# A decoder layer on one core: the up projection's outputs in two sets, each tile convolved a tile later, a copy on another engine, four row-by-row steps at the end

## The chip, the core and the metric

The kernel runs on one core of a Trainium2 chip. The core has a matrix engine, TensorE (PE in the profile, its weight loads PEld), and three engines for elementwise work: VectorE (DVE), ScalarE (ACT) and GpSimd (POOL). SyncE (SP) issues nearly all transfers between the chip's memory and the core's on-chip memory; a matmul's result lands in one of eight accumulator banks, from which DVE or ACT fetch it. Each engine works through its own instructions in order and waits on semaphores for the others. The metric is the time of one execution in microseconds, the median of three runs.

## The reference

One layer of a hybrid decoder in float32, on 1024 tokens behind 16 meta tokens, with 1024 columns: a combined input projection, four heads of differential attention and four heads of a gated linear recurrence, an output projection, and then a feed-forward part with a convolution, which is most of the work:

```python
def conv_ffn(a, w_up, conv_w, conv_b, w_down):
    u = a @ w_up                                  # 1024 -> 2 * 2816
    u = lax.conv_general_dilated(u, conv_w[:, None, :], window_strides=(1,),
        padding=[(CONV_WIDTH - 1, 0)], dimension_numbers=('NWC', 'WIO', 'NWC'),
        feature_group_count=C) + conv_b           # 3 taps along the tokens
    gate, up = jnp.split(u, 2, axis=-1)
    return (jax.nn.gelu(gate, approximate=True) * up) @ w_down

    # in the layer
    mix = jnp.concatenate([y_diff, y_hgrn], axis=-1) @ w_out[l]
    h = h + rmsnorm(mix, ln_mix_post[l])
    a = rmsnorm(h, ln_ffn_pre[l])
    h = h + rmsnorm(conv_ffn(a, ...), ln_ffn_post[l])
```

In the attention, each block of 128 queries forms two softmaxes p0 and p1 over the keys so far, and (p0 − λ·p1) is multiplied by the values.

## The kernel before

**Precision and products.** Each operand of a float32 product is split into a high part, cast to a fast 32-bit matmul type by ACT, and a low remainder, which DVE or POOL form by subtraction. A product is then three matmuls, high by high, high by low, low by high: L1412 to L1414 in the up phase, L1586 to L1588 in the down phase. Both phases use a 2 × 2 block scheme with seven block products in place of eight.

**Stages.** Up to about 490 us the input projections run between the heads: a projection, an attention head's blocks and the recurrence's steps are generators that a planner interleaves. Until 646 us the output projection, its norm and the transposed, split tokens follow. Then come 22 tiles of the up phase (ft = 0 to 21, each 128 gate columns and 128 up columns), to 1064.85 us, and last the down phase, 77 steps: seven products in the order 1, 2, 5, 6, 3, 7, 4 of 11 steps each, a step being four rows of three matmuls with 512 columns.

**A tile of the up phase.** `unit(ft, p)` is a generator with one yield for each of its seven products, and two units, p = 0 and 1 for the two token halves, run side by side. Product j of a unit is 12 matmuls into one of three banks in turn: pa, pb, pc, pb, pa, pb, pc. What fetches a bank is named by its result: ACT copies pa to x1 (in the profile xu) and to ug; DVE adds pb to x1 for u2 (xu), pb to x1 for u3 (u), pc to u3 and pb to x1 for the two halves of uu, pc to u2 for the second half of ug. `outputs(ft, p)` gives the buffers ug and uu (gate and up); `gated` convolves them: for each side, `conv` runs one ACT instruction and two scalar-tensor-tensor instructions on DVE (c<-ug and c<-uu), then ACT makes the GELU, POOL multiplies the two sides, and SP stores the row block to gsc in the chip's memory. `later` is a list of tiles' halves that are still to be convolved; the loop over ft takes one from it at j = 1 and one at j = 3, behind that product's last addition (an order edge, `issue_after`, that only sets the order on one engine).

In the kernel before, tiles 1 and 2 take their outputs from buffers that the down phase owns (tags gk, gh, gl) and leave their convolutions to the next tile; tile 3 and all later ones take them from the pool xu and convolve at their own end, at j = 6. Tile 0, which is made in a plain way, leaves its convolutions to tile 1.

Beside this, `prep` makes the next tile's weights: `load_raw4` loads four blocks ra, POOL forms sums of them (ws), ACT casts the high parts uh, and DVE and POOL form the low ones ul.

**Down phase.** `operands` loads (gi from gsc, wi from the weights) and splits both into gh, gl, wh, wl, three steps ahead. The first three pairs of loads (`opens`) are issued in tile 20, at j = 5, behind the last gsc store so far, and split in tile 21. For products 1 to 7 all four rows (m = 0 to 3, one bank each) are summed step by step; in the last one, product 4, the last `TAIL` steps are done row by row, so that row 0 can be fetched, normed and stored while the others are still summed. `evac` does that: a subtraction from the bank on DVE, the squares and the root on ACT, a multiplication by the gain and one or two scalar-tensor-tensor instructions into hh on DVE, for rows 0 to 2 also one addition on POOL, and a store of the row block.

**Attention.** `values(i)` transposes the softmax block i in pieces of four 128-blocks to a bank (pt) and copies each piece to the tile at, by DVE or ACT in turn; `apply(i)` multiplies them by the values (L746).

**Order.** PE's matmuls keep the order in which the program writes them. The other engines' instructions are put in order by a scheduler, so a diff of a few lines can move many of them. All elementwise instructions are recorded under one helper's line, L58; they are told apart by their tiles.

Of the kernel before, what the change touches and what calls it, by code (L numbers as in the profile page):

```python
# [9 lines left out]
F32 = mybir.dt.float32  # L10
# [7 lines left out]
P = 128  # L18
# [3 lines left out]
D = 1024  # L22
KD = D // P
DFF = 2816
NF = DFF // P
HEADS = 4
NBLK = 9
# [63 lines left out]
def layer_kernel(ctx: ExitStack, tc: tile.TileContext, x, meta, table, lbl, gpre, gpost, win,  # L91
# [3 lines left out]
    V, A = Ordered(tc, nc.vector, state), Ordered(tc, nc.scalar, state)  # L95
# [552 lines left out]
    def attn(h, tens):  # L648
# [60 lines left out]
        def values(i):  # L709
            r = rows(i)  # L710
            q0 = start(i)
            W = q0 + r
            nm = f"{h}_{i}"
            pb = pend.pop(i)
            pieces = [list(range(j, min(j + 4, i + 1))) for j in range(0, i + 1, 4)]
            ats = []
            for pi, blks in enumerate(pieces):
                pt = ps_m(f"pt{nm}_{pi}")
                at = ap_.tile([P, len(blks) if pi == 2 else 4, P], F32, tag=f"at{pi // 2}", name=f"at{nm}_{pi}", bufs=2 - pi // 2)
                for jj, j in enumerate(blks):  # L720
                    b = rows(j) if i == 0 else P
                    T.transpose(pt[:b, jj * r:(jj + 1) * r], pb[:r, 0, start(j):start(j) + b], ident[:r, :r])
                pv = pt.rearrange("p (j q) -> p j q", j=4)[:, :, :r] if r == P else None
                n0 = len(blks)
                if pi == 0:
                    A.copy(az[i % 2][:META, :r], pt[:META, :r])
                lo = 1 if pi == 0 else 0
                if n0 > lo:
                    (A.copy if pi % 2 else V.tensor_copy)(at[:, lo:n0], pv[:, lo:n0])
                ats.append(at)  # L730
                yield 0.8 if i < 4 else 0.6
            pend["ats"] = ats, pieces
# [323 lines left out]
        return mix_tile(tag, F32R, f"mp{n}_{i}")[:, : 2 * KD * P].rearrange("p (l k t) -> p l k t", l=2, k=KD)  # L1056

    def block_load(m, i, k0, k1):
        SY.dma_start(m[:, :, k0:k1].bitcast(F32).rearrange("p l k t -> p l (k t)"), msc[i][:, :, P * k0:P * k1])

    def first_load(i):
        blocks[i] = block_tile(0, i)
        block_load(blocks[i], i, 0, 4)
        block_load(blocks[i], i, 4, 7)

    def second_load(i):
        blocks[i] = block_tile(1, i)
        block_load(blocks[i], i, 0, 4)
        block_load(blocks[i], i, 4, 7 if i == 1 else 8)

    blocks = {}
    first_load(1)
    first_load(2)
    wo0 = load_wo(0)
    wo0_loaded = last_load[-1]
    SY.dma_start(gpo0, gpost[:, :512].to_broadcast([P, 512]))

    def y0_gain(p):
# [59 lines left out]
    def load_raw4(ft):  # L1138
        raws.clear()
        for nm, m, c in (("11", ft, 0), ("22", ft + NF, 1), ("21", ft + NF, 0), ("12", ft, 1)):  # L1140
            raws[nm] = swp.tile([P, 512], F32, tag="ra", name=f"ra{ft}_{nm}", bufs=5)
            with tc.issue_after(wo0_loaded.ins):
                SY.dma_start(raws[nm], wup[m][:, 512 * c: 512 * (c + 1)])

    def w_sum(nm, a, b, op):
# [208 lines left out]
    gap(tp, "gap1", 128)  # L1354

    def outputs(ft, p):
        if ft in (1, 2):
            if p == 0:
                return [dn.tile([P, 2 * WN[0]], F32, tag="gk", name=f"{t}{ft}_{p}") for t in ("ug", "uu")]
            return [dn.tile([P, 512], F32R, tag=g, name=f"{t}{ft}_{p}").bitcast(F32) for g, t in (("gh", "ug"), ("gl", "uu"))]  # L1360
        return [xup.tile([P, 2 * WN[0]], F32, tag=t, name=f"{t}{ft}_{p}") for t in ("ug", "uu")]
# [35 lines left out]
    def unit(ft, p, bank):  # L1397
        n = WN[p]
        nm = f"{ft}_{p}"
        ug, uu = outputs(ft, p)  # L1400
        if (ft, p) == (1, 0):
            gap(dn, "gap7", 384)
        pair = mxp.tile([P, 768], F32, tag="ms", name=f"xu_{nm}", bufs=2)
        x1, u2 = pair[:, :n], pair[:, WN[0]:WN[0] + n]
        u3 = xup.tile([P, WN[0]], F32, tag="u3", name=f"u3_{nm}")[:, :n]

        def mm(j, pt, first):
            hi, lo = made[7 * ft + j]
            th, tl = tt[p][j]
            for k in range(4):  # L1410
                s = slice(P * k, P * (k + 1))
                T.matmul(pt, hi[:, s], th[:, k], start=(first and k == 0), stop=False, skip_group_check=True)  # L1412
                T.matmul(pt, hi[:, s], tl[:, k], start=False, stop=False, skip_group_check=True)  # L1413
                T.matmul(pt, lo[:, s], th[:, k], start=False, stop=(k == 3), skip_group_check=True)  # L1414

        pa = bank(f"pa{nm}")[:, :n]
        mm(0, pa, True)
        marks["x1"] = A.copy(x1, pa)
        yield
        pb = bank(f"pb{nm}")[:, :n]  # L1420
        mm(1, pb, True)
        marks[ft, p] = marks["last"] = V.tensor_tensor(u2, pb, x1, op=ALU.add)
        yield
        pc = bank(f"pc{nm}")[:, :n]
        mm(2, pc, True)
        yield
        mm(3, pb, False)
        V.tensor_tensor(u3, pb, x1, op=ALU.add)
        marks["last"] = V.tensor_tensor(uu[:, n:2 * n], pc, u3, op=ALU.add)
        yield  # L1430
        mm(4, pa, False)
        marks["left"] = A.copy(ug[:, :n], pa)
        yield
        mm(5, pb, False)
        marks["last"] = V.tensor_tensor(uu[:, :n], pb, x1, op=ALU.add)
        yield
        mm(6, pc, False)
        marks["last"] = V.tensor_tensor(ug[:, n:2 * n], pc, u2, op=ALU.add)
        if ft in (1, 2):
            later.append((ft, p, ug, uu))  # L1440
        else:
            gated(ft, p, ug, uu)
        yield
# [87 lines left out]
    for ft in range(1, NF):  # L1531
        units = [unit(ft, p, ps_b) for p in range(2)]
        for j in range(7):
            if j != 1:
                with tc.issue_after(marks["gain"].ins) if ft == 1 else nullcontext():
                    prep(7 * (ft + 1) + j)
            for u in units:
                next(u)
            if ft < 4 and j in (1, 3):
                with tc.issue_after(marks["last"].ins):  # L1540
                    gated(*later.pop(0))
            if j == 1:
                prep(7 * (ft + 1) + j)
            if ft == NF - 2 and j == 5:
                with tc.issue_after(marks["store"].ins):
                    opens = [(g_in(k, 0, "1"), w_in(1, k)) for k in range(LOOK)]
            if ft == NF - 1 and 1 < j < 5:
                with tc.issue_after(marks["x1"].ins), tc.issue_after(marks[ft, 1].ins):
                    ready[j - 2] = operands(1, j - 2, opens[j - 2])
    close(t2_cm, t_cm, xu_cm, mx_cm)  # L1550

    f_cm, fp = pool("fin", 1)
    TAIL = 3
    keep.update({nm: fp.tile([P, NH, 512], F32, tag=nm, name=nm) for nm in ("ga", "gb", "gc", "gs")})
    c11 = fp.tile([P, 4, 512], F32, tag="c11", name="c11")
    x5 = fp.tile([P, 4, 512], F32, tag="x5", name="x5")
# [49 lines left out]
    def evac(pr, m, py):  # L1606
# [7 lines left out]
        elif pr == 5:  # L1614
            A.copy(x5[:, m], py)
        elif pr == 6:
            V.tensor_tensor(u2[:, m], py, x1[:, m], op=ALU.subtract)
        elif pr == 3:
            c = u2[:, m]
            V.tensor_tensor(c, c, py, op=ALU.subtract)  # L1620
            squares(c, m, 1)
            s_ = rstd(m, 1)
            hh = fp.tile([P, D], F32, tag="hh", name=f"hh{m}", bufs=2)
            SY.dma_start(hh, hsc[P * m: P * (m + 1), :])
            V.scalar_tensor_tensor(hh[:, :512], c11[:, m], s_, hh[:, :512], ALU.mult, ALU.add)
            G.tensor_tensor(c, c, gfo[:, 512:], op=ALU.mult)
            V.scalar_tensor_tensor(hh[:, 512:], c, s_, hh[:, 512:], ALU.mult, ALU.add)
            SY.dma_start(out[P * m: P * (m + 1), :], hh)
        elif pr == 7:
            V.tensor_tensor(x1[:, m], py, x1[:, m], op=ALU.subtract)  # L1630
            c = x5[:, m]
            V.tensor_tensor(c, x1[:, m], c, op=ALU.subtract)
            squares(c, 4 + m, 1)
            as_bias(4 + m, 1)
            G.tensor_tensor(c, c, gfo[:, 512:], op=ALU.mult)
        else:
            c = x1[:, m]
            V.tensor_tensor(c, py, c, op=ALU.subtract)
            squares(c, 4 + m, 0)
            V.tensor_tensor(c, c, gfo[:, :512], op=ALU.mult)  # L1640
            s_ = rstd(4 + m, 0)
            hh = hhs[m]
            V.scalar_tensor_tensor(hh[:, :512], c, s_, hh[:, :512], ALU.mult, ALU.add)
            if m == 3:
                V.scalar_tensor_tensor(hh[:, 512:], x5[:, m], s_, hh[:, 512:], ALU.mult, ALU.add)
            else:
                A.mul(x5[:, m], x5[:, m], s_)
                G.tensor_tensor(hh[:, 512:], hh[:, 512:], x5[:, m], op=ALU.add)
            SY.dma_start(out[P * (4 + m): P * (5 + m), :], hh)

    for i, (pr, k) in enumerate(steps):
        ahead(i + LOOK)
# [85 lines left out]
```

## Time and profile before

| | us |
|---|---|
| median of 3 runs | 1288.24 |
| lowest, highest | 1287.69, 1289.94 |
| the profiled execution, its own time | 1287.61 |
| its span, first to last instruction | 1285.5 |
| mean granted PE clock in it | 0.997 |

The profile gives for each engine the busy time, and for groups of instructions the mean time of one and what ended the idle time before them ("<- DVE xu L58" is an instruction on DVE that wrote xu). Windows cut the span into stretches, with the busy time of each engine in each, the granted clock of PE and the share of time in which the transfer engines were busy. Rows of the timeline begin with the start and the duration, both in us; what stands in brackets is idle time just before the instruction and what ended it.

### The profile page before, as it was taken

To read this page: it belongs to the slowest core of one execution; us is meant where nothing else is said; L and a number is where in the kernel's file an instruction comes from. 1 tells how busy PE (TensorE), PEld (TensorE's weight loads), DVE (VectorE), ACT (ScalarE), POOL (GpSimd) and SP (SyncE) were. 2 spreads that over 40 slices of the span, in tenths; PEclk is the share of its full clock that TensorE was granted. 3 is DMA by queue.
4 is the path that set the end of the run, shared out by engine and by line. 5 is a ranking of instruction groups with operands and counts; after the bars stand their busy time and mean duration, and the time that the engine had idled before them with its cause. 6 is when DMAs were issued, how large, how long until landed. Compare 5 with 4: busy or idle time off the path is not lost.

```text
span 1285.5 us, 26038 instructions
## 1 busy us (share of the span) xinstructions
PE 1258.9 (98%) x10154; PEld 1175.4 (91%) x10154; DVE 887.8 (69%) x1485; ACT 691.9 (54%) x1639; POOL 492.2 (38%) x390
## 2 busy tenths in 40 slices
PE   8999999999999999999999899999999999999996
PEld 7999999999999998778999899999999998888885
DVE  7564646465646564557899778778778776797686
ACT  8475466546654754356763544444445444464543
POOL 5231423242323311353067576676676630010121
PEclk9999999999999999999999999999999999999999
DMA  7235555273734533788322222222222147955263
GB/s 258 95 62 129 88 141 93 79 145 95 127 92 80 124 84 111 226 276 266 117 67 75 83 86 80 75 90 84 75 80 86 66 155 237 346 172 167 88 213 123
DMA packets 116417, 165.04 MB, mean 128 GB/s; under 512 B 10099, under 2 KB 57523, under 8 KB 116294
## 3 DMA queue, kind: packets, MB, share of 16 engines
q1 hardware_dynamic: 93062, 151.84, 36.2%
q0 software_dynamic: 23232, 11.54, 7.7%
q8 instruction: 80, 1.31, 0.4%
q14 instruction: 43, 0.35, 0.1%
HBM read 134.24 MB, written 52.17 MB: 145 GB/s over the span
## 4 chain that ended last, share of the span: by engine, by line
PE 44%; DVE 5%; issue 2%; ACT 2%; POOL 1%; DMA 0%; DVEq 0%; POOLq 0%; ACTq 0%
PE pd L1587 5%; PE pd L1588 5%; PE pd L1586 5%; PE pb L1412 4%; PE pb L1413 4%; PE pb L1414 4%; PE pa L1413 3%; PE pa L1412 3%; PE pa L1414 3%; PE pc L1413 3%; PE pc L1412 3%; PE pc L1414 3%; DVE c L58 2%; DVE xh L58 1%; POOL ws L58 1%
## 5 line engine op out<-in xcount | busy, mean ns | idle before, releaser
L1412 PE MATMUL pb<-t,uh 128*128 128x258 f32 x504 | 141.4, 281 | 4.6 <-DVE xu L58 3.8
L1413 PE MATMUL pb<-t,uh 128*128 128x258 f32 x504 | 141.7, 281 | 0.4 <-DVE t L58 0.4
L1414 PE MATMUL pb<-t,ul 128*128 128x258 f32 x504 | 140.9, 280 | 0.0
L1587 PE MATMUL pd<-wl,gh 128*128 128x512 f32 x308 | 120.2, 390 | 0.7 <-DVE wl L58 0.7
L1586 PE MATMUL pd<-wh,gh 128*128 128x512 f32 x308 | 119.9, 389 | 0.0
L1588 PE MATMUL pd<-wh,gl 128*128 128x512 f32 x308 | 119.8, 389 | 0.0
L58 DVE SCALAR_TENSOR_TENSOR c<-uu,cwt,c 128x514 f32<-128x514 f32 (+1 forms) x88 | 98.0, 1114 | 18.9 <-ACT c L58 18.3
L58 POOL TENSOR_TENSOR c<-c,c 128x514 f32<-128x514 f32 (+1 forms) x44 | 64.8, 1473 | 113.0 <-ACT c L58 111.0
L1412 PEld LDWEIGHTS pb<-t,uh 128*128 128x128 f32 x504 | 95.6, 190 | 4.9 <-DVE xu L58 4.0
L1413 PEld LDWEIGHTS pb<-t,uh 128*128 128x128 f32 x504 | 95.6, 190 | 0.6 <-DVE t L58 0.6
L1414 PEld LDWEIGHTS pb<-t,ul 128*128 128x128 f32 x504 | 95.5, 190 | 0.0
L1413 PE MATMUL pa<-t,uh 128*128 128x258 f32 (+1 forms) x336 | 93.9, 279 | 0.0
L1413 PE MATMUL pc<-t,uh 128*128 128x258 f32 (+1 forms) x336 | 93.9, 279 | 0.0
L1412 PE MATMUL pa<-t,uh 128*128 128x258 f32 (+1 forms) x336 | 93.6, 279 | 0.0
L1412 PE MATMUL pc<-t,uh 128*128 128x258 f32 (+1 forms) x336 | 93.6, 278 | 0.0
L1414 PE MATMUL pa<-t,ul 128*128 128x258 f32 (+1 forms) x336 | 93.4, 278 | 0.0
L1414 PE MATMUL pc<-t,ul 128*128 128x258 f32 (+1 forms) x336 | 93.4, 278 | 0.0
L58 POOL TENSOR_TENSOR ul<-ws,uh 128x512 fp32r<-128x512 f32 x42 | 65.2, 1552 | 72.5 <-PE pa L1414 43.9
L58 DVE SCALAR_TENSOR_TENSOR c<-ug,cwt,c 128x514 f32<-128x514 f32 (+1 forms) x88 | 89.2, 1013 | 0.9 <-ACT c L58 0.3
L58 ACT CAST uh<-ra 128x512 fp32r<-128x512 f32 x67 | 41.2, 617 | 61.2 <-PE pb L1413 36.2
L58 DVE TENSOR_TENSOR ul<-ra,uh 128x512 fp32r<-128x512 f32 x43 | 40.4, 941 | 46.1 <-ACT uh L58 41.2
L1587 PEld LDWEIGHTS pd<-wl,gh 128*128 128x128 f32 x308 | 57.8, 188 | 13.9 <-DVE wl L58 2.1
(389 smaller groups left out, 4169.1 us busy)
## 6 DMA issues: line engine op xcount, KB each, us to landing
ra<-in_wup_dram SPq DMA_DIRECT2D x88, 256.0 KB, 2.7
mp<-msc SPq DMA_DIRECT2D x23, 512.0 KB, 5.1
tsc<-in_wdown_dram SPq DMA_DIRECT2D x44, 256.0 KB, 4.8
wi<-tsc SPq DMA_DIRECT2D x44, 256.0 KB, 3.1
gi<-gsc SPq DMA_DIRECT2D x33, 256.0 KB, 4.1
wi<-in_wdown_dram SPq DMA_DIRECT2D x33, 256.0 KB, 4.6
gsc<-c SPq DMA_DIRECT2D x22, 257.0 KB, 2.0
tsc<-in_wdown_dram POOLq DMA_DIRECT2D x22, 256.0 KB, 7.0
```

The source lines that it names most:

```text
L58: ins = call(*args, **kw)
L1412: T.matmul(pt, hi[:, s], th[:, k], start=(first and k == 0), stop=False, skip_group_check=True)
L1413: T.matmul(pt, hi[:, s], tl[:, k], start=False, stop=False, skip_group_check=True)
L1414: T.matmul(pt, lo[:, s], th[:, k], start=False, stop=(k == 3), skip_group_check=True)
L1586: T.matmul(py, gh[:, s], wh, start=(k == 0 and pr not in (3, 7)), stop=False, skip_group_check=True)
L1587: T.matmul(py, gh[:, s], wl, start=False, stop=False, skip_group_check=True)
L1588: T.matmul(py, gl[:, s], wh, start=False, stop=(k == NH - 1), skip_group_check=True)
```

## The change

- `outputs`: tile 1 and every even tile take their outputs from the down phase's buffers, the other tiles from the pool xu.
- `unit`: every tile but the last leaves its convolutions to the next tile; the loop takes one from the list at j = 1 and one at j = 3 in every tile. The last tile, 21, convolves the halves of tile 20 there and its own at its end.
- `values`: in the next to last query block of each head the second piece is copied by DVE, no longer by ACT.
- `load_raw4`: its loads are put behind a load of the output projection's fourth block, no longer behind the last load of the output weights.
- `TAIL` is 4, no longer 3, and the last row block is stored in two halves, the second half of its columns first.

```diff
@@ values
-                    (A.copy if pi % 2 else V.tensor_copy)(at[:, lo:n0], pv[:, lo:n0])
+                    (A.copy if pi % 2 and i != NBLK - 2 else V.tensor_copy)(at[:, lo:n0], pv[:, lo:n0])
@@ block_load, first_load, load_raw4
-        SY.dma_start(m[:, :, k0:k1]...
+        return SY.dma_start(m[:, :, k0:k1]...
-        block_load(blocks[i], i, 4, 7)
+        loaded[i] = block_load(blocks[i], i, 4, 7)
-            with tc.issue_after(wo0_loaded.ins):
+            with tc.issue_after(loaded[4].ins):
                 SY.dma_start(raws[nm], wup[m][:, 512 * c: 512 * (c + 1)])
@@ outputs
-        if ft in (1, 2):
+        if ft == 1 or ft and ft % 2 == NF % 2:
@@ unit
-        if ft in (1, 2):
+        if ft < NF - 1:
             later.append((ft, p, ug, uu))
         else:
             gated(ft, p, ug, uu)
@@ the loop over ft
-            if ft < 4 and j in (1, 3):
+            if j in (1, 3):
                 with tc.issue_after(marks["last"].ins):
                     gated(*later.pop(0))
@@ the down phase
-    TAIL = 3
+    TAIL = 4
@@ evac
-            SY.dma_start(out[P * (4 + m): P * (5 + m), :], hh)
+            for c0 in (512, 0) if m == 3 else (0,):
+                c1 = c0 + 512 if m == 3 else D
+                SY.dma_start(out[P * (4 + m): P * (5 + m), c0:c1], hh[:, c0:c1])
```

Three places of the printed order show what the scheduler makes of it. The first is DVE from the end of tile 3 into tile 4. Names carry the tile and the half (uu3_0: tile 3, half 0); c0 is the gate's side of a convolution and c1 the up's, ul a weight's low part, xu_4_0 tile 4's second step, u2. Before:

```order
L58 TENSOR_TENSOR uu3_1_8544<-pb3_1_8575,xu_3_1_8545 128x256
L58 SCALAR_TENSOR_TENSOR c1_3_0_8765<-uu3_0_8526,cwt_84,c1_3_0_8765 128x514
L58 TENSOR_TENSOR ug3_0_8525<-pc3_0_8610,xu_3_0_8527 128x258
L58 SCALAR_TENSOR_TENSOR c1_3_1_8789<-uu3_1_8544,cwt_84,c1_3_1_8789 128x510 x2
L58 SCALAR_TENSOR_TENSOR c0_3_0_8760<-ug3_0_8525,cwt_84,c0_3_0_8760 128x514
L58 TENSOR_TENSOR ug3_1_8543<-pc3_1_8623,xu_3_1_8545 128x256
L58 TENSOR_TENSOR ul35_8806<-ra5_11_8795,uh35_8805 128x512
L58 SCALAR_TENSOR_TENSOR c0_3_1_8784<-ug3_1_8543,cwt_84,c0_3_1_8784 128x510 x2
L58 TENSOR_TENSOR xu_4_0_8811<-pb4_0_8845,xu_4_0_8811 128x258
```

Now:

```order
L58 TENSOR_TENSOR uu3_1_8544<-pb3_1_8575,xu_3_1_8545 128x256
L58 TENSOR_TENSOR ug3_0_8525<-pc3_0_8610,xu_3_0_8527 128x258
L58 TENSOR_TENSOR ug3_1_8543<-pc3_1_8623,xu_3_1_8545 128x256
L58 TENSOR_TENSOR ul35_8784<-ra5_11_8773,uh35_8783 128x512
L58 TENSOR_TENSOR xu_4_0_8789<-pb4_0_8823,xu_4_0_8789 128x258
L58 TENSOR_TENSOR ul36_8865<-ws2_8862,uh36_8864 128x512
L58 TENSOR_TENSOR xu_4_1_8807<-pb4_1_8837,xu_4_1_8807 128x256
L58 SCALAR_TENSOR_TENSOR c0_3_0_8851<-ug3_0_8525,cwt_84,c0_3_0_8851 128x514
L58 SCALAR_TENSOR_TENSOR c1_3_0_8856<-uu3_0_8526,cwt_84,c1_3_0_8856 128x514
```

The eight convolution instructions of tile 3 stood ahead of tile 4's second step; now the first of them stands behind it.

The second place is SP's queue around the up phase's end: the stores of tile 21's two halves to gsc, and loads of the down phase (gfo a gain, gc and ga blocks kept for later products, gi5_12 a block of product 5, gi1_7 and gi1_8 the gated rows of steps 7 and 8). Before:

```order
L1377 DMA gsc_90<-c0_21_0_13468 128x514
L1489 DMA gi5_12_13615<-gsc_90 128x512
L1561 DMA gfo_13516<-in_gfpost_dram 128x1024
L1377 DMA gsc_90<-c0_21_1_13492 128x510
L1564 DMA gc_13512<-gsc_90 128x512
L1567 DMA ga_13510<-gsc_90 128x512
L1489 DMA gi1_7_13631<-gsc_90 128x512
L1489 DMA gi1_8_13655<-gsc_90 128x512
```

Now:

```order
L1376 DMA gsc_90<-c0_21_0_13468 128x514
L1560 DMA gfo_13516<-in_gfpost_dram 128x1024
L1376 DMA gsc_90<-c0_21_1_13492 128x510
L1563 DMA gc_13512<-gsc_90 128x512
L1566 DMA ga_13510<-gsc_90 128x512
L1488 DMA gi5_12_13615<-gsc_90 128x512
L1488 DMA gi1_7_13631<-gsc_90 128x512
L1488 DMA gi1_8_13655<-gsc_90 128x512
```

The load of gi5_12 moved from before the last store to between it and the loads of steps 7 and 8. (The second pair of gc and ga loads, which stands between in both, is left out.)

The third place is DVE at the program's end, where pd4_m is the bank of row m in product 4 and hh4 the rows that are stored. Before, from row 2's bank on (its first rows end row 1):

```order
L58 TENSOR_TENSOR x1_13518<-pd4_2_15225,x1_13518 128x512
L58 SCALAR_TENSOR_TENSOR hh4_15227<-x1_13518,ssd_13517,hh4_15227 128x512
L58 TENSOR_TENSOR x1_13518<-x1_13518,gfo_13516 128x512
L58 TENSOR_TENSOR x1_13518<-pd4_3_15226,x1_13518 128x512
L58 SCALAR_TENSOR_TENSOR hh4_15227<-x1_13518,ssd_13517,hh4_15227 128x512
L58 TENSOR_TENSOR x1_13518<-x1_13518,gfo_13516 128x512
L58 SCALAR_TENSOR_TENSOR hh4_15227<-x5_13515,ssd_13517,hh4_15227 128x512
L58 SCALAR_TENSOR_TENSOR hh4_15227<-x1_13518,ssd_13517,hh4_15227 128x512
```

Now:

```order
L58 TENSOR_TENSOR x1_13518<-pd4_2_15225,x1_13518 128x512
L58 TENSOR_TENSOR x1_13518<-x1_13518,gfo_13516 128x512
L58 SCALAR_TENSOR_TENSOR hh4_15227<-x1_13518,ssd_13517,hh4_15227 128x512
L58 TENSOR_TENSOR x1_13518<-pd4_3_15226,x1_13518 128x512
L58 TENSOR_TENSOR x1_13518<-x1_13518,gfo_13516 128x512
L58 SCALAR_TENSOR_TENSOR hh4_15227<-x5_13515,ssd_13517,hh4_15227 128x512
L58 SCALAR_TENSOR_TENSOR hh4_15227<-x1_13518,ssd_13517,hh4_15227 128x512
```

Row 2's last instruction stood behind row 3's subtraction and now stands ahead of it, as do the rows before.

More of the change, by code (lines that the diff above doesn't have):

```diff
@@ L1058, in block_load @@
     def block_load(m, i, k0, k1):
-        SY.dma_start(m[:, :, k0:k1].bitcast(F32).rearrange("p l k t -> p l (k t)"), msc[i][:, :, P * k0:P * k1])
+        return SY.dma_start(m[:, :, k0:k1].bitcast(F32).rearrange("p l k t -> p l (k t)"), msc[i][:, :, P * k0:P * k1])
     def first_load(i):
@@ L1069, in second_load @@
         block_load(blocks[i], i, 4, 7 if i == 1 else 8)
-    blocks = {}
+    blocks, loaded = {}, {}
     first_load(1)
@@ L1074, in layer_kernel @@
     wo0 = load_wo(0)
-    wo0_loaded = last_load[-1]
     SY.dma_start(gpo0, gpost[:, :512].to_broadcast([P, 512]))
```

## The prediction

> **What bounds the kernel now.** I read the busy times first, then what TensorE (PE) waits for, then the up phase cut at its tiles' first matmuls, and last the rows around each wait.
>
> ```profile
> PE 1258.9 (98%) x10154; PEld 1175.4 (91%) x10154; DVE 887.8 (69%) x1485; ACT 691.9 (54%) x1639; POOL 492.2 (38%) x390
> PE pb L1412 <- DVE xu L58: 3.8, 1, 3.8
> PE pa L746 <- ACT at L58: 2.9, 4, 1.2
> 687.56:707.11 19.55, 19.55 (x170) 19.55 (x169) 17.03 (x24) 9.32 (x18) 14.01 (x9) 1.00 0.25 82
> 707.11:732.28 25.17, 21.40 (x170) 21.20 (x169) 18.69 (x29) 12.31 (x22) 16.11 (x12) 0.93 0.27 95
> 720.20:723.70 3.50, 3.50 (x19) 3.50 (x19) 1.87 (x4) 0.53 (x2) 3.50 (x3) 0.51 0.22 77
> 719.43 0.39 PE L1412 MATMUL pb<-t,uh 128*128 128x258 f32 x1 [3.77 <-DVE xu L58]
> ```
>
> PE is busy for 98% of the span. The change takes no matmul away, so all that it can win is PE's idle time, matmuls run at a lowered clock, and what follows the last matmul. The first two window rows are tiles 3 and 4 of the up phase (length, PE, PEld, DVE, ACT, POOL, granted clock, DMA share, GB/s). Tile 4 takes 25.17 us, tile 3 19.55: 5.62 too many. The gap of 3.77 before one matmul is the first part; the other, 5.62 − 3.77 = 1.85, is the clock, since in the 3.5 us behind the gap the granted clock was 0.51, and half speed for 3.5 us loses some 1.75.
>
> **Part 1: outputs in two sets, the convolutions a tile later.** VectorE (DVE) is late by that gap because one tile holds too much: before, tile 2 leaves its two convolutions to tile 3, and tile 3 does its own at its end too. Its last rows before the gap:
>
> ```profile
> 716.62 2.42 DVE L58 SCALAR_TENSOR_TENSOR c<-ug,cwt,c 128x510 f32<-128x510 f32 x2
> 718.96 0.41 DVE L58 TENSOR_TENSOR xu<-pb,xu 128x258 f32<-128x258 f32 x1
> ```
>
> The addition xu<-pb at 718.96 is tile 4's second step; the bank pb cannot be written again before it. In the order of the change nothing of tile 3's convolutions stands ahead of it: they come in tile 4, four instructions behind the additions of product 1, four behind those of product 3. No instruction is added, so the eight are spread over the tile, and the gap with its clock should go: −5.6.
>
> [...]
>
> Tiles 2 and 3 of before already run in the order that the change gives to tiles 4 to 20, on all engines, so they price it:
>
> ```profile
> 669.39 0.41 DVE L58 TENSOR_TENSOR uu<-pb,xu 128x258 f32<-128x258 f32 x1
> 708.13 0.41 DVE L58 TENSOR_TENSOR uu<-pb,xu 128x258 f32<-128x258 f32 x1
> 677.04 0.74 DVE L58 SCALAR_TENSOR_TENSOR c<-ug,cwt,c 128x514 f32<-128x514 f32 x1
> 677.71 1.79 DVE L58 SCALAR_TENSOR_TENSOR c<-uu,cwt,c 128x514 f32<-128x514 f32 x1
> 677.64 1.31 POOL L58 TENSOR_TENSOR ws<-ra,ra 128x512 f32<-128x512 f32 x1 [3.67 <-DMA ra<-in_wup_dram]
> 681.12 0.41 DVE L58 TENSOR_TENSOR u<-pb,xu 128x258 f32<-128x258 f32 x1
> 681.97 0.28 PE L1412 MATMUL pb<-t,uh 128*128 128x258 f32 x1
> 696.42 0.74 DVE L58 SCALAR_TENSOR_TENSOR c<-ug,cwt,c 128x514 f32<-128x514 f32 x1
> 696.53 1.79 POOL L58 TENSOR_TENSOR ws<-ra,ra 128x512 f32<-128x512 f32 x1 [3.18 <-DVE c L58]
> 700.50 0.41 DVE L58 TENSOR_TENSOR u<-pb,xu 128x258 f32<-128x258 f32 x1
> 701.52 0.28 PE L1412 MATMUL pb<-t,uh 128*128 128x258 f32 x1
> ```
>
> PE had no gap in these tiles. The tightest place is the addition u<-pb of product 3, which ends at 681.53 for a matmul at 681.97 (0.44 to spare), and a tile later at 700.91 for 701.52 (0.61). The addition uu<-pb comes round every (708.13 − 669.39) / 2 = 19.37 us, less than PE's 19.55, so DVE gains 0.18 a tile and the pattern should hold: 0 for tiles 5 to 20.
>
> The same rows show the danger. A convolution instruction takes 0.74 alone and 1.79 beside GpSimd's (POOL's) sum ws<-ra,ra; today one of the four meets it, and the third ended just ahead of the sum (it began 0.60 and 0.11 behind the third's start). One more that meets it costs 1.04 a tile, above the spare time.
>
> [...]
>
> **The end of the up phase.** Tile 20's eight convolution instructions now come in tile 21, beside tile 21's own eight and the first operands of the down phase.
>
> ```profile
> 1051.40:1070.90 19.50, 19.50 (x144) 18.43 (x143) 16.53 (x28) 9.30 (x17) 3.21 (x2) 1.00 0.44 144
> 1070.12 0.74 DVE L58 SCALAR_TENSOR_TENSOR c<-ug,cwt,c 128x510 f32<-128x510 f32 x1
> 1075.33 3.26 SPq L1489 DMA_DIRECT2D gi<-gsc x3
> 1081.03 0.62 ACT L58 CAST gh<-gi 128x512 fp32r<-128x512 f32 x1 [4.58 <-DMA gi<-gsc]
> 1064.69:1083.75 19.06, 19.06 (x87) 15.77 (x86) 14.06 (x21) 8.94 (x16) 2.89 (x2) 1.00 0.71 231
> ```
>
> DVE is idle for 19.50 − 16.53 = 2.97 there, and eight instructions add 8 × 0.67 = 5.4 (0.67 is the step between two such starts, 677.04 to 677.71). So the last convolution, 1070.12 before, should come some 5.4 − 2.97 = 2.4 later, less what DVE finds free behind it; I take 2, and the store that follows it, on SP's queue ahead of the loads of step 7, about 1.8. The order shows one load more moved in ahead of them, gi5_12; at 0.5 to 0.7 each (the three loads at 1075.33 took 3.26 of the queue) they are 2.3 to 2.5 later. The gated rows of step 7, cast at 1081.03 before, are then cast at about 1083.4, and their low part follows by one 0.67 instruction: 84.1 to 84.5. Seven steps of the down phase end at 1083.75, so step 7 may wait 0.4 to 0.7; I take +0.7, with 0 (the loads overlap as before) and 2.5 (nothing overlaps) as ends. Tile 21's own additions stand ahead of its convolutions, so I put no gap at PE before that.
>
> **Part 2: one of the transposes' copies on DVE.** The waits' second row says 2.9 us in four waits, one for each attention head. One of them:
>
> ```profile
> 238.77 0.58 ACT L58 COPY at<-pt 128x512 f32<-128x512 f32 x1
> 237.42 0.83 PE L746 MATMUL pa<-avn,at 128*128 128x128 f32 x6
> 239.40 1.16 PE L746 MATMUL pa<-avn,at 128*128 128x128 f32 x8 [1.15 <-ACT at L58]
> 236.20 0.56 DVE L58 COPY at<-pt 128x384 f32<-128x384 f32 x1 [0.25 <-ACT az L58]
> 236.67 0.71 DVE L58 TENSOR_TENSOR ast<-ast 128x1 f32<-128x1 f32 x1
> 238.91 0.16 DVE L58 TENSOR_TENSOR ast<-ast 128x1 f32<-128x1 f32 x1 [1.53 <-ACT pb L58]
> ```
>
> ScalarE (ACT) copies at<-pt at 238.77, and PE waits 1.15 for it. DVE sits idle from 237.38 for 1.53. By the order the copy follows the ast instruction of 236.67 there. The like copy of 384 columns took 0.56 at 236.20, so 512 take about 0.56 × 512 / 384 = 0.75 at most, until 238.13; the matmuls in front of the waiting eight end at 238.25. Hidden: −2.9. What DVE has behind waits for an exponential until 238.91, so nothing else is late, and ACT gains 0.58. If the copy met another late DVE row in half of the heads, −1.4; the other end is −2.9, as there is no more to win.
>
> **Part 3: up weights' loads.** Their order edge moves to another load of the same queue; in the printed order the SP instructions around them stand as before, as do their waits. 0, and no end worth naming.
>
> **Part 4: four last steps row by row, and the last rows stored in two halves.**
>
> ```profile
> 1269.87 0.69 DVE L58 TENSOR_TENSOR x<-pd,x 128x512 f32<-128x512 f32 x1 [3.04 <-PE pd L1588]
> 1272.56 0.74 DVE L58 SCALAR_TENSOR_TENSOR hh<-x,ssd,hh 128x512 f32<-128x512 f32 x1
> 1275.56 0.39 PE L1588 MATMUL pd<-wh,gl 128*128 128x512 f32 x1
> 1277.22 0.68 DVE L58 TENSOR_TENSOR x<-pd,x 128x512 f32<-128x512 f32 x1
> 1277.82 1.80 DVE L58 SCALAR_TENSOR_TENSOR hh<-x,ssd,hh 128x512 f32<-128x512 f32 x1
> 1280.15 1.40 DVE L58 SCALAR_TENSOR_TENSOR hh<-x,ssd,hh 128x512 f32<-128x512 f32 x2
> 1274.47 7.44 SPq L1649 DMA_DIRECT2D out_dram<-hh  x4
> out_dram<-hh SPq DMA_DIRECT2D x8, 512.0 KB, 2.6
> gsc<-c SPq DMA_DIRECT2D x22, 257.0 KB, 2.0
> ```
>
> The last matmul ends at 1275.95, DVE starts the last subtraction at 1277.22, 1.27 late, because it is behind with earlier rows, and its last instruction ends at 1281.55, 5.60 behind PE. Seven steps of the down phase take 19.06 (the window above), one 2.72; four steps of one row are as many matmuls as one step of all four rows, so the rows end 2.72 apart instead of 2.04 with three, and in the new order each row is finished before the next. From the first subtraction to the end of its hh, without the next row's subtraction between (0.60), is 1273.30 − 1269.87 − 0.60 = 2.83, about the distance of the rows, so the last row should start at once: 1275.95 + 2.83 = 1278.8, plus the second hh of 0.7 and some contention with POOL: 1279.8, a gain of 1.7. The last store is 256 KB, not 512: 2.0 against 2.6 to land by the two DMA rows, though halves issued together share the engines: 0 to 0.6 more, I take 0.3. In all −2.0; bounds −0.7 (the halves cost an issue and POOL still meets the last rows) and −2.4.
>
> **Sum.** −5.6 + 0.7 − 2.9 + 0 − 2.0 = −9.8. The profiled execution took 1287.61 (its span 1285.5), so 1277.8; the median shown, 1288.24, lies 0.63 above it, and the forecast against it is **1278.4 us**. The terms' own ends give 1276 to 1281.5.
>
> **The rivals.**
> (a) *The overload only moves to tile 21.* There DVE has sixteen convolution instructions and the first splits, as tile 3 has today; then a gap like 3.77 with its 1.85 comes back at the end. For: 2.97 idle against 5.4 added. Against: tile 21's additions stand ahead of its own convolutions, and behind the up phase PE needs only splits. It gives 1278.4 + 5.6 = 1284.0.
> (b) *Slower: POOL meets a second convolution instruction in every tile.* Place: product 3 of tiles 4 to 20; price: DVE's round becomes 19.37 + 1.04 = 20.41, 0.86 above PE's, so 17 tiles lose 14.6 less the spare 0.5: 1278.4 + 14.1 = 1292.5. It decides against the change from 9.8 / 17 = 0.58 a tile. For: the margin was 0.60, then 0.11 us. Against: in the second of these tiles the spare time grew, and POOL's sum was itself released by that convolution.
> (c) *The gains at the copies and the tail are taken up* by the waits behind them (ACT's chain, the stores' landing): 1278.4 + 2.9 + 1.3 = 1282.6.
> (d) *The weights' loads do not move at all*, as I read the order: no other time, since that part is already at 0.
>
> **How the numbers follow.** Forecast 0.70, (a) 0.12, (c) 0.10, (b) 0.08. The forecast's own range 1276.0 to 1281.5 grows to 1284.5 to take in (c) and most of (a); outside lie (b), a part of (a) and some 5 in 100 of the forecast. About 0.2%, 2.6 us here, is what this kernel's measurement can tell from no change: faster is a time below 1285.6. The forecast and (c) lie there, as does most of (a): 0.87. Same takes the rest of (a) and a mild (b): 0.06. Slower is (b): 0.07.
>
> **What would show it.** Right: tile 4 takes 19.55, at a clock of 1.00; no wait L1412 <- xu; no wait L746 <- ACT at; DVE's last instruction ends 3.9 behind the last matmul, not 5.6; a wait of under 2.5 near step 7 of the down phase at the most. Wrong: tiles of over 19.6 in a row, with two convolution instructions at 1.8 each (b); a gap in tile 21 or behind (a); a gap where the copy was, now released by DVE (c). A wait in the down phase that I have not priced, on transfers that now collide, would also break the sum.

## The result and the profile after

| | before | changed |
|---|---|---|
| median of the runs, us | 1288.84 (6 runs) | 1277.66 (6 runs) |
| lowest, highest | 1287.59, 1289.94 | 1276.64, 1281.14 |
| ratio, 95% interval | | 0.9919 (0.9904 to 0.9934) |

The changed kernel is faster by 11.2 us, where 9.8 were forecast; its median is 0.7 below the forecast of 1278.4. Cut into four stages, the two profiled executions compare like this (starts of tile 1, end of tile 21, end of the last matmul, end of the span):

| stage, us | before | changed | difference | predicted |
|---|---|---|---|---|
| start to tile 1's first matmul | 646.65 | 642.93 | −3.72 | −2.9 |
| tiles 1 to 21 | 418.20 | 412.53 | −5.67 | −5.6 |
| down phase to the last matmul | 211.09 | 211.86 | +0.77 | +0.7 |
| last matmul to the end | 9.56 | 7.55 | −2.01 | −2.0 |
| span | 1285.5 | 1274.9 | −10.6 | −9.8 |

The busy times of the changed kernel, and four of the rows of what PE waits for (total, times, longest):

```profile
PE 1256.4 (99%) x10154; PEld 1172.8 (92%) x10154; DVE 914.5 (72%) x1489; ACT 687.2 (54%) x1635; POOL 507.8 (40%) x390
PE pl L477 <- issue: 1.9, 1, 1.9
PE pa L1249 <- DVE a L58: 1.2, 2, 0.7
PE pd L1586 <- DVE wl L58: 0.9, 3, 0.4
PE pb L1411 <- DVE u L58: 0.8, 1, 0.8
```

Both waits that the change was costed on, pb for DVE's xu and L746 for ACT's at, are gone from the list; no wait of the up phase's tiles 2 to 21 is in it. DVE is busy for 26.7 us more (887.8 before) though it has only four instructions more, the copies, 2.7 us in all. Most of it is in the convolution instructions, of which 80 now take over 1.2 us and 67 did before: they meet POOL more often, at the price of 1.79 against 0.74, and PE does not feel it. Tiles 4 and 17 in windows (length, PE, PEld, DVE, ACT, POOL, clock, DMA share, GB/s):

```profile
703.34:722.89 19.55, 19.55 (x170) 19.55 (x169) 17.03 (x23) 9.41 (x18) 13.74 (x9) 1.00 0.24 82
957.53:977.08 19.55, 19.55 (x170) 19.55 (x169) 16.91 (x23) 9.31 (x17) 13.47 (x10) 1.00 0.26 82
```

Tile 4 has lost its 5.62 us, at full clock. Tile 17 is one of the two in which the slower rival's event took place:

```profile
965.04 1.81 DVE L58 SCALAR_TENSOR_TENSOR c<-ug,cwt,c 128x514 f32<-128x514 f32 x1
966.77 1.79 DVE L58 SCALAR_TENSOR_TENSOR c<-uu,cwt,c 128x514 f32<-128x514 f32 x1
965.01 1.29 POOL L58 TENSOR_TENSOR ws<-ra,ra 128x512 f32<-128x512 f32 x1 [3.25 <-DMA ra<-in_wup_dram]
970.19 0.41 DVE L58 TENSOR_TENSOR u<-pb,xu 128x258 f32<-128x258 f32 x1
```

POOL's sum began 0.03 ahead of the third convolution instruction, so two of the four took 1.8. The addition for product 3 came 1.07 later in its tile than in the tiles around it, still in time, and POOL was through with its own work earlier too: the last two convolution instructions of the tile then ran alone, 0.73 each, where they take 1.77 and 0.74 in the other tiles.

The place in the second head that showed the wait of 1.15, and the tail:

```profile
235.84 0.71 DVE L58 TENSOR_TENSOR ast<-ast 128x1 f32<-128x1 f32 x1
236.47 0.68 DVE L58 COPY at<-pt 128x512 f32<-128x512 f32 x1
236.59 1.78 PE L746 MATMUL pa<-avn,at 128*128 128x128 f32 x14
...
1266.93 0.39 PE L1587 MATMUL pd<-wh,gl 128*128 128x512 f32 x1
1267.35 0.75 DVE L58 SCALAR_TENSOR_TENSOR hh<-x,ssd,hh 128x512 f32<-128x512 f32 x1
1268.02 0.68 DVE L58 TENSOR_TENSOR x<-pd,x 128x512 f32<-128x512 f32 x1
1269.50 0.69 DVE L58 TENSOR_TENSOR x<-x,gfo 128x512 f32<-128x512 f32 x1 [0.79 <-ACT sq L58]
1270.13 1.42 DVE L58 SCALAR_TENSOR_TENSOR hh<-x,ssd,hh 128x512 f32<-128x512 f32 x2
```

The fourteen matmuls of L746 run through in 1.78; before, the same fourteen took from 237.42 to 240.56, 3.14. The copy took 0.68 on DVE, in its idle time. In the tail PE ends at 1267.32, DVE's last instruction at 1271.55, 4.23 later (5.60 before), and the span 3.32 after that (3.96 before).

### The profile page after: what moved, and what is told of

The parts are those of the page before. It is cut to its first block, busy times and chain, and to the rows that moved or that the text cites. A ratio compares the mean times of both kernels' runs of the same rounds, so it can differ in the third digit from the quotient of the medians.

```text
span 1274.9 us, 26032 instructions
## 1 busy us (share of the span) xinstructions
PE 1256.4 (99%) x10154; PEld 1172.8 (92%) x10154; DVE 914.5 (72%) x1489; ACT 687.2 (54%) x1635; POOL 507.8 (40%) x390
## 4 chain that ended last, share of the span: by engine, by line
PE 48%; DVE 3%; DMA 1%; ACT 1%; issue 1%; POOL 1%; DVEq 0%; SPq 0%; ACTq 0%; POOLq 0%
PE pd L1586 5%; PE pd L1587 5%; PE pd L1585 5%; PE pb L1412 4%; PE pb L1411 4%; PE pb L1413 4%; PE pa L1412 3%; PE pc L1412 3%; PE pa L1411 3%; PE pc L1411 3%; PE pc L1413 3%; PE pa L1413 3%; PE pq L1390 1%; PE pq L1389 1%; PE pq L1391 1%
## 5 line engine op out<-in xcount | busy, mean ns | idle before, releaser
L58 DVE SCALAR_TENSOR_TENSOR c<-uu,cwt,c 128x514 f32<-128x514 f32 (+1 forms) x88 | 107.0, 1215 | 0.0
L58 DVE SCALAR_TENSOR_TENSOR c<-ug,cwt,c 128x514 f32<-128x514 f32 (+1 forms) x88 | 101.4, 1153 | 0.0
L58 ACT ACTIVATE c<-c 128x514 f32<-128x514 f32 (+1 forms) x44 | 27.9, 634 | 124.7 <-DVE c L58 124.7
L58 POOL TENSOR_TENSOR ws<-ra,ra 128x512 f32<-128x512 f32 x42 | 69.2, 1648 | 61.8 <-DMA ra<-in_wup_dram 31.4
L58 POOL TENSOR_TENSOR ul<-ws,uh 128x512 fp32r<-128x512 f32 x42 | 69.1, 1646 | 60.0 <-PE pa L1413 44.2
L58 POOL TENSOR_TENSOR c<-c,c 128x514 f32<-128x514 f32 (+1 forms) x44 | 67.9, 1543 | 52.6 <-ACT c L58 49.2
```

The costliest lines, as they stand in the source:

```text
L58: ins = call(*args, **kw)
```

## The experiments

Each run of a job stands beside runs of the kernel before on the same chip. The stages of the profiled executions, in us, are those of the table above:

| kernel | to tile 1 | tiles 1 to 21 | down phase | tail | median, ratio to before (interval) |
|---|---|---|---|---|---|
| e1, part 1 alone | 647.45 | 412.97 | 212.69 | 9.58 | 1284.12, 0.9951 (0.9938 to 0.9965) |
| e2, part 2 alone | 642.85 | 419.36 | 212.13 | 9.57 | 1284.98, 0.9960 (0.9948 to 0.9973) |
| e3, part 4 alone | 646.24 | 418.18 | 212.13 | 7.54 | 1286.49, 0.9977 (0.9967 to 0.9987) |
| e4, part 3 alone | 648.40 | 419.56 | 211.61 | 9.57 | 1289.09, 0.9999 (0.9990 to 1.0007) |
| e8, changed again | 640.13 | 412.58 | 212.72 | 7.55 | 1276.19, 0.9900 (0.9886 to 0.9915) |
| e10, changed again | 642.49 | 412.52 | 212.29 | 7.55 | 1276.41, 0.9901 (0.9887 to 0.9914) |
| e9, three edits more | 643.08 | 415.79 | 211.58 | 7.37 | 1277.54, 0.9910 (0.9897 to 0.9924) |
| e11, two edits more | 641.59 | 412.97 | 212.28 | 7.35 | 1276.90, 0.9906 (0.9891 to 0.9920) |
| e12, no halves | 643.00 | 412.97 | 211.75 | 8.18 | 1278.43, 0.9913 (0.9896 to 0.9930) |

### e1 to e4: each part by itself

**e1**, the kernel before with the edits of `outputs`, `unit` and the loop:

```diff
-        if ft in (1, 2):
+        if ft == 1 or ft and ft % 2 == NF % 2:
...
-        if ft in (1, 2):
+        if ft < NF - 1:
...
-            if ft < 4 and j in (1, 3):
+            if j in (1, 3):
```

> The kernel before with part 1 alone (outputs in two sets, convolutions a tile later). My theory: the whole of tile 4's loss goes, so the up phase's 21 units take 412.5 us in place of 418.2 (tile 4 19.55 at a granted clock of 1.00); at most 0.7 is given back in the down phase; in all 4.9 to 5.7 us faster than before, about 1283. Rival 1 (the round of DVE gets longer when GpSimd meets a second convolution instruction): single tiles above 19.6 and under 3 us gained. Rival 2 (the overload moves to tile 21): a gap of 1 us or more at tile 21 or in the first eight steps of the down phase.

Measured: 1284.12 against 1289.16, 5.0 us faster; tiles 1 to 21 take 412.97. No tile but the first is longer than 19.6. My theory holds for the up phase. Its bound of 0.7 for the down phase does not: that took 1.60 more than in the profile of before, 0.98 of it at steps 6 and 7, which is what is left of rival 2, and most of the rest at step 25 (see below). None of it is in tile 21.

**e2**, the kernel before with the copy on DVE:

```diff
-                    (A.copy if pi % 2 else V.tensor_copy)(at[:, lo:n0], pv[:, lo:n0])
+                    (A.copy if pi % 2 and i != NBLK - 2 else V.tensor_copy)(at[:, lo:n0], pv[:, lo:n0])
```

> The kernel before with part 2 alone (the copy on DVE in the next to last query block). My theory: the four waits of L746 for ACT's at are gone, with the restart behind each: 2.9 to 3.9 us faster, and the up phase starts that much earlier. Rival: the heads' gain is taken up by the waits behind them before the up phase (520 to 650 us), and under 1.5 us are left.

Measured: 4.2 us faster; tile 1 starts 3.80 earlier than in the profile of before. By the profile my theory holds at its upper end, beyond the sum of the recorded waits, 2.93; by the medians the gain is a little above my range (3.5 to 6.7 by the interval). That run's tile 4 shows another thing. Its window, and the stretch in it in which PE was granted half its clock:

```profile
703.30:729.63 26.33, 22.56 (x170) 22.36 (x169) 18.47 (x29) 12.32 (x22) 16.11 (x12) 0.87 0.29 91
714.83:721.66 6.83, 6.05 (x28) 6.05 (x29) 3.89 (x9) 2.28 (x4) 5.62 (x5) 0.50 0.24 88
```

The gap is 3.77 as in before, but half clock lasts 6.83 us, twice 3.41, and tile 4 takes 26.33 in place of 25.17. So the loss in tile 4 is not one number: 5.6 with one such stretch of 3.41, 6.8 with two.

**e3**, the kernel before with `TAIL = 4` and the last rows' halves:

```diff
-    TAIL = 3
+    TAIL = 4
...
-            SY.dma_start(out[P * (4 + m): P * (5 + m), :], hh)
+            for c0 in (512, 0) if m == 3 else (0,):
+                c1 = c0 + 512 if m == 3 else D
+                SY.dma_start(out[P * (4 + m): P * (5 + m), c0:c1], hh[:, c0:c1])
```

> The kernel before with part 4 alone (four row-by-row steps, last rows stored in halves). My theory: from the last matmul to the end of the span 7.6 us in place of 9.55, 2.0 faster in all. Rival: the four steps' operands come late and stall PE in the last four steps, so that under 1 us is left.

Measured: 2.7 us faster (1.7 to 4.3 by the interval), tail 7.54. No wait of PE in the last four steps: my theory, not the rival.

**e4**, the kernel before with the up weights' order edge moved:

```diff
-            with tc.issue_after(wo0_loaded.ins):
+            with tc.issue_after(loaded[4].ins):
```

> The kernel before with part 3 alone (the up weights' loads behind another load). My theory: no instruction moves, within 0.5 us of before. Rival: the first tile's weights come earlier and take the gap of 0.78 us in tile 1 away, 0.8 us faster; or they crowd the output projection's loads, and it is slower by as much.

Measured: 1289.09 against 1289.16. Tile 1's wait for u is 0.80, as before. Part 3 does nothing that can be measured. The medians of e1 to e4 add up to −12.0 us, the whole change has −11.2: within the intervals, the parts do not stand in each other's way.

### e5 to e7: what makes the gap

**e5**, the changed kernel with the overload put at tile 11:

```diff
-        if ft < NF - 1:
+        if ft < 11:
             later.append((ft, p, ug, uu))
...
-            if j in (1, 3):
+            if later and j in (1, 3):
```

> The changed kernel, but tiles 11 to 21 convolve at their own end again, so that tile 11 holds four convolutions (the two of tile 10 and its own two), as tile 3 did before. My theory (the gap is the overload, wherever it lies): tiles 4 to 11 take 19.55, and tile 12 has one gap of 3.8 at its second product with one or two stretches of half clock behind it, 25.2 or 26.2 us; about 6 us slower than the changed kernel. Rival (the gap belongs to the place: the first tiles' weights or loads): tile 4 is long again, or no tile is.

Measured: 1280.23 (two runs), 4.0 above the changed kernel's 1276.19 of the same job (e8). Tiles 11 and 12, and the matmul behind the gap:

```profile
838.17:857.73 19.56, 19.56 (x171) 19.56 (x169) 16.93 (x23) 9.30 (x17) 13.54 (x10) 1.00 0.25 82
857.73:881.57 23.84, 21.40 (x170) 21.20 (x169) 17.27 (x27) 11.54 (x20) 15.42 (x12) 0.93 0.26 89
868.71 0.39 PE L1411 MATMUL pb<-t,uh 128*128 128x258 f32 x1 [2.44 <-DVE xu L58]
```

The gap went with the overload: same bank, same releaser, tile 12, and tile 4 is at 19.55. That is the cause of tile 4's loss shown. Its size was wrong: 2.44, not 3.8. By tile 11 DVE had run ahead: its first convolution instruction came 7.55 us into tile 3 and 6.18 into tile 11, and 7.55 − 6.18 = 1.37 is about what is missing from 3.77 (1.33).

**e6**, the same with three convolutions in tile 11 and three in tile 12:

```diff
-        if ft < 11:
+        if ft < 11 or ft == 11 and p == 1:
             later.append((ft, p, ug, uu))
```

> As the run before, but tile 11 leaves one of its two convolutions to tile 12, so that tiles 11 and 12 hold three each. [...]

Measured: 1282.47, 6.3 above the changed kernel of the same job, with a gap of 3.53 in tile 12, longer than that of e5, and a lowered clock with it: 0.93 over the 25.01 us from 860.14 to 885.15. My estimate, 3.8 less four instructions of 0.7 to 1.1, was a gap of about 1 at most; it failed. The rows ahead of the gap on DVE, and the matmul:

```profile
869.76 1.72 DVE L58 SCALAR_TENSOR_TENSOR c<-ug,cwt,c 128x510 f32<-128x510 f32 x1
871.41 1.77 DVE L58 SCALAR_TENSOR_TENSOR c<-uu,cwt,c 128x510 f32<-128x510 f32 x1
873.10 1.77 DVE L58 SCALAR_TENSOR_TENSOR c<-ug,cwt,c 128x510 f32<-128x510 f32 x1
874.80 0.74 DVE L58 SCALAR_TENSOR_TENSOR c<-uu,cwt,c 128x510 f32<-128x510 f32 x1
877.40 0.41 DVE L58 TENSOR_TENSOR u<-pb,xu 128x258 f32<-128x258 f32 x1
877.87 0.39 PE L1411 MATMUL pb<-t,uh 128*128 128x258 f32 x1 [3.53 <-DVE u L58]
```

With tile 11's other half convolved at the start of tile 12 as well, both halves stood ahead of product 3's addition. So the number of convolutions in a tile does not tell the gap here (2.44 in e5, 3.53 in e6); it matters which addition they stand in front of. That tile still held more than eight convolution instructions; e7 keeps the number at eight.

**e7**, the changed kernel with both of the convolutions at product 1:

```diff
-            if j in (1, 3):
+            if j == 1:
                 with tc.issue_after(marks["last"].ins):
                     gated(*later.pop(0))
+                    gated(*later.pop(0))
```

> The changed kernel with both convolutions of the tile before taken at product 1 (eight instructions in a row ahead of product 3's additions, in place of four and four). My theory (what a tile has to spare is the distance from product 3's addition to the matmul that needs its bank, 0.4 to 2 us): four more instructions of 0.7 to 1.8 us make that addition late by 1 to 4 us in every tile, PE waits for u there, 20 to 70 us slower than the changed kernel. Rival (only the sum of DVE's work in a tile counts, and it is the same): within 3 us of the changed kernel.

Measured: 1352.51, 76 us slower than the changed kernel of the same job, above my range; the rival (the same sum of work) is out by far. The wait, and two stretches that each begin behind a gap of 2.09:

```profile
PE pb L1411 <- DVE u L58: 46.1, 21, 6.5
735.59:740.25 4.66, 4.66 (x26) 4.66 (x27) 2.98 (x6) 1.70 (x4) 3.69 (x3) 0.63 0.34 114
759.13:763.79 4.66, 4.66 (x39) 4.66 (x40) 3.43 (x7) 2.26 (x5) 3.98 (x4) 1.00 0.33 112
```

46.1 us are the waits; what I had not counted is half clock behind most of them, 16 stretches in the trace's clock records; the run's mean clock was 0.977. Both windows are 4.66 long and PE is busy throughout; at a clock of 0.63 it ran 26 matmuls, at 1.00 it ran 39. The tile around the first of these gaps, 717.00 to 740.50, takes 23.50 at a clock of 0.93, 3.95 above 19.55: 2.09 for the gap and 1.86 that came with it.

### e8 and e10: the changed kernel again

> The changed kernel once more, for the spread of its runs. My theory: its slow runs carry one or two half-clock stretches of 3.4 us behind a wait that the profiled execution did not have; median 1277 to 1279, and if the profile shows such a run, a half-clock stretch with a gap of over 3 us ahead of it. Rival: the spread lies in the projections' start or the down phase's loads, at full clock.

> The changed kernel on the same chip, to stand beside the run before: 1276 to 1279, whichever theory is right.

Measured: e8 1274.76 to 1279.42, e10 1275.20 to 1277.09; the run of 1279.42 had a mean clock of 0.999, so my theory of the spread does not hold for it. The profiles of the changed kernel and of those that are alike up to tile 1 but for the loads (e2) or in full (e5 to e7, e12) start tile 1 at 640.1 to 643.6, with a wait "pl <- issue" in the recurrence at about 518 us that is absent in e8, 1.9 in the first profile and 2.2 in e10. In e12 that wait was 1.63, and the stretch behind it ran at 0.50:

```profile
516.01:519.42 3.41, 1.78 (x71) 1.52 (x71) 0.79 (x2) 0.00 (x0) 0.00 (x0) 1.00 0.86 280
519.42:522.83 3.41, 3.41 (x21) 2.19 (x23) 0.78 (x3) 0.00 (x0) 0.00 (x0) 0.50 0.08 26
```

PE's matmuls stand in the same order in all these kernels, so their starts can be compared one by one: against e8 this one place costs from 0.6 us (e5) to 2.5 (e7), and 3.1 in e12, with the half clock. It is not the only one: in e6 about 1.5 more are lost between 490 and 505 us. What makes the wait long or short in a run stays open; the slowest runs of the first comparison (1280.23 and 1281.14 at 0.997 and 0.995) have no trace.

### e9 and e11: a version beyond the changed kernel

**e9** adds three edits to the changed kernel; **e11** has the second and third alone:

```diff
@@ (1) the loop over ft
-            if j in (1, 3):
+            if j in ((3, 5) if ft == 1 else (1, 3)):
@@ (2) the down phase's loads and sums
-        early.setdefault(min(3 + 3 * k, 2 * NH - 3 + k), []).append(k)
+        early.setdefault(8 if k == 1 else min(3 + 3 * k, 2 * NH - 3 + k), []).append(k)
...
+        with tc.issue_after(marks["wl", 5, 3].ins) if k > 8 else nullcontext():
             V.tensor_tensor(keep["gs"][:, k], b, keep["gc"][:, k], op=ALU.subtract)
@@ (3) evac of product 4: the last instructions of row m, now in finish(m)
         evac(4, m, banks[4][m])
+        if m:
+            finish(m - 1)
+    finish(3)
...
+            with tc.issue_after(marks["sub", min(m + 1, 3)].ins):
                 V.scalar_tensor_tensor(hh[:, :512], c, s_, hh[:, :512], ALU.mult, ALU.add)
```

> The changed kernel with three more edits, each for a wait that its trace still shows. (1) Tile 0's convolutions in tile 1 are taken at products 3 and 5, not 1 and 3: product 3's addition is no longer late there, tile 1 takes 20.3 us or less in place of 21.3. (2) The second load for the sums of product 5 is issued two steps later and the last two of these sums stand behind the weights' low part of product 5, step 3: the waits at steps 6, 7 and 25 of the down phase (0.3 to 1.0 and 0.5 to 1.5 over the runs) go, 211.0 us from the up phase's end to the last matmul in place of 211.9 to 212.7. (3) In the tail each row's last instruction stands behind the next row's subtraction: the last subtraction starts 0.1 us behind the last matmul in place of 0.7, 6.9 to 7.1 us from it to the end in place of 7.55. My theory (each wait is set by what stands ahead on DVE): 2.5 to 3.5 us faster than the changed kernel of the same job. Rival (the work comes late at the next place: tile 2's second product, or the rows of the tail in the order of the kernel before): one of the three stages is not shorter, and under 1.5 us are gained.

> The run with three more edits without its first (tile 0's convolutions in tile 1 back at products 1 and 3). My theory (that edit alone cost the run its gain, by the gap in tile 2): tile 1 21.3, tile 2 19.55 at full clock, 211.0 to 211.6 us of the down phase to the last matmul and 7.37 us of tail; 0.9 us faster than the changed kernel by its stages, too little for the ratio to show surely: 0.989 to 0.990 of the kernel before. Rival (something else made that run slow): a stage longer than in the changed kernel's runs, or a ratio above 0.991.

Measured: e9 1277.54 beside 1276.41 for the changed kernel on the same chip: not faster. Its first two tiles:

```profile
643.08:663.40 20.32, 19.97 (x170) 19.77 (x169) 18.76 (x24) 13.04 (x22) 17.08 (x8) 1.00 0.19 54
663.40:687.19 23.79, 21.58 (x170) 21.23 (x169) 22.31 (x27) 9.61 (x18) 15.74 (x11) 0.93 0.25 79
```

Tile 1 won 1.0 as expected and tile 2 lost 4.2, to a gap of 2.21 and half clock (0.50 from 679.89 to 683.30): the work came late at the next place, the rival's case. e11 confirms it: without that edit tile 2 is at 19.55. Edit 2 took the waits at steps 6 and 7 away in both runs, but not that at step 25 (0.48 and 1.20), so that the down phase of e11 is no shorter than that of e10. Edit 3 let the last subtraction start at once, and gained only 0.2: the instruction behind it took 1.39 in place of 0.75, by my estimate because it now met POOL's addition, which lasts 1.26 to 1.30 in the changed kernel. e11's ratio, 0.9906, cannot be told from 0.9901 of the changed kernel. No version beat it.

### e12: the halves

```diff
-            for c0 in (512, 0) if m == 3 else (0,):
-                c1 = c0 + 512 if m == 3 else D
-                SY.dma_start(out[P * (4 + m): P * (5 + m), c0:c1], hh[:, c0:c1])
+            SY.dma_start(out[P * (4 + m): P * (5 + m), :], hh)
```

> The changed kernel with the last row block stored whole. My theory (the halves win what a store of 256 KB lands earlier than one of 512 KB, 2.0 against 2.6 us): 8.1 to 8.2 us from the last matmul to the end in place of 7.55. Rival (the halves share the transfer engines and win nothing): 7.5 to 7.7.

Measured: tail 8.18, 0.63 more. DVE's last instruction ends 4.23 us behind PE as in the changed kernel, so all of it is the store.

## Why the prediction was right

**Part 1, −5.6.** Right in place, mechanism and size: −5.67 by the profile, −5.0 by the medians of e1, which hold the loss in the down phase too, and e5 moved the gap with its cause. That 5.6 is one of two values (25.2 and 26.2 us for tile 4 over the profiles of before, e2, e3 and e4) I could not see in one trace.

**The danger of POOL, rival (b).** The event came true in tiles 17 and 19 and cost PE nothing. The step that was wrong in the rival is "DVE's round becomes 20.41": in tile 17, as in tile 4, four of the eight convolution instructions are slow (1.45 to 1.81, the others 0.73 to 0.75); in tiles 17 and 19 one more of the early ones took 1.8 and one fewer of the late ones. The prediction also misread its two rows: the third instruction had not ended ahead of POOL's sum (it ran from 677.04 to 677.78, the sum from 677.64). It had begun first, and ran at 0.74; in tile 17 the sum began first, by 0.03, and the instruction took 1.81. Besides, the spare time had grown: DVE ran ahead by about 0.2 a tile, as the round of 19.37 said, until tile 11, where it waits for PE.

**Rival (a)** did not come: tile 21 shows no gap in any profile. The reason given against it holds: its additions stand ahead of its own convolutions, and e6 and e7 show that this position is what counts.

**Rivals (c) and (d).** (c) did not come either: alone, the copies still win 3.80 up to tile 1 (e2) and the tail 2.0 (e3). (d) gives no other time than the forecast, and e4 measures none.

**The end of the up phase, +0.7.** The place was right. Counted from the end of tile 21, the last store was issued 1.52 later than before and the loads of steps 7 and 8 2.00 later, where I had 1.8 and 2.3 to 2.5; the load moved in took 0.44 of the queue, and my 0.5 to 0.7 for it does not follow from the row that I gave (3.26 for three loads). The size at step 7 was 0.30 in the first profile, 0.98 with step 6 in e1, 0.56 in e8 and 0.41 in e10. The two rows behind the first of these, on DVE and PE:

```profile
1074.23 2.08 DVE L58 TENSOR_TENSOR gl<-gi,gh 128x512 fp32r<-128x512 f32 x3 [0.62 <-ACT gh L58]
1074.97 0.50 PE L1587 MATMUL pd<-wh,gl 128*128 128x512 f32 x1
```

The low part came at 1074.91, 0.55 behind the step's start at 1074.36, as forecast; but only the step's third matmul needs it, which is due 0.45 into the step, so less of it reached PE, 0.30 over the step. The rest of the +0.77 is the wait at step 25, 0.54 there and 0.08 in the profile of before; since e2 to e4, which have the old up phase and one other part each, lose 0.59 to 1.13 at it, it is not a cost of part 1, and no single part explains it; what sets it from run to run stays open. The agreement of the sum is partly luck.

**Part 2, −2.9.** Mechanism right, term mis-sized: −3.9 at the four waits (e1 against the changed kernel's first profile, from 40 matmuls ahead of each wait to 40 behind: 0.55, 1.37, 1.36 and 0.61), −4.2 by e2's medians. "There is no more to win" was wrong: the recorded idle time starts at the modelled end of the matmul before, while the unhindered matmuls of L746 start before that end (they last 0.28 and start 0.11 apart), and the first one behind a wait takes 0.21 to the next start. From start to start each wait costs 0.24 more, 0.96 in all. The rest of the first stage gave 0.2 back, within what profiles of the same kernel differ by there (see e8).

**Part 3, 0.** Right, by e4.

**Part 4, −2.0.** The sum is right (−2.01), its terms are not: 1.37 from the rows and 0.63 from the halves (e12), where I had 1.7 and 0.3. "The last row should start at once" failed: the rows come 2.94 apart on DVE (1265.09 to 1268.02 between two subtractions) against 2.72 on PE, because DVE stands for 0.79 in each, waiting for ACT's square, so the last subtraction started 0.70 late, and DVE's last instruction ended 4.23 behind PE, not 3.9.

## What to carry to other kernels

Before moving work to a later tile, find the first instruction on that engine that PE's next use of a bank waits for, and count what stands in front of it: the same eight instructions in each tile cost nothing as four and four and 76 us as eight. Cost a PE wait from start to start, and look at the granted clock behind it: here tiles with half clock lost 1.9 to 3.0 us beyond their gaps of 2.1 to 3.8. A neighbour tile that already runs in the new order is the best price list there is.

## What the runs showed of the hardware

In some stretches PE was granted half its clock. The records show 0.50 from 720.24 to 723.65 in before, from 519.42 to 522.83 in e12 and from 679.89 to 683.30 in e9, each 3.41 us long, and from 714.83 to 721.66 in e2, 6.83, twice that. In before, the 3.41 us ahead held 0.81 us of busy PE:

```profile
716.83:720.24 3.41, 0.81 (x6) 0.81 (x7) 3.38 (x5) 1.97 (x6) 2.02 (x2) 1.00 0.44 156
720.24:723.65 3.41, 3.41 (x18) 3.41 (x17) 1.83 (x4) 0.49 (x1) 3.41 (x3) 0.50 0.22 78
```

In e2 the gap of 3.77 ran on into the halved stretch, by 0.78: PE was busy for 6.05 of the 6.83. Shorter gaps had a lowered clock with them too: 3.53 in e6, 2.44 in e5, 2.21 in e9 and one of 2.09 in e7 (733.50 to 735.59, then 0.63 over 4.66 us). Another gap of 2.09 in e7 (757.04 to 759.13) had not: 1.00 over the 4.66 us behind it. In e12 the 3.41 us ahead of the halved stretch had only 1.63 of idle PE. So the length of a gap did not tell alone whether half clock followed; what does is not shown.

Beyond the length of its gap, a tile with half clock lost 1.85 us in before and in e5 (tiles of 25.17 and 23.84 against 19.55), 1.86 in e7, 1.93 in e6, 2.03 in e9, and 3.01 in e2 with the longer stretch. Tile 4 is the same code in before and in e2, and its gap is 3.77 in both; it took 25.17 in one and 26.33 in the other, so the same code differed by 1.16 with the half clock alone.
